# Where the searches for the 256 keys stand in a two-layer attention trunk

## The chip, the core and the metric

The kernel runs on one core of one Trainium2 chip. The metric is device time in microseconds (us). Before the change three runs took 4272.74, 4274.78 and 4277.41 us; their median is 4274.78 us. TensorE is called PE here, VectorE DVE, ScalarE ACT, GpSimd POOL, and SP issues all DMAs.

## What is computed

The reference is two layers of one mixer over 2048 tokens of width 1024. Each layer normalises its rows, projects them, feeds four head groups of width 256 and maps their gated results back:

```python
h = rms_norm(x, ln_g)
proj = jnp.einsum('bsd,dn->bsn', h, w_in)
y_a = stick_breaking(a_q, a_k, a_v)                    # group A
y_b = softmax_attention(q_b, k_b, v_b, MLA_QK ** -0.5) # group B, latent attention
y_c = dsa_attention(qc, kc, c_v, iq, ik, iw, topk)     # group C, 256 chosen keys
y_d = rms_norm(diff_attention(...), diff_subln_g) * (1.0 - lam_init)  # group D
x = x + einsum(concat(silu(gate) * y), w_out)
```

In group C the keys of a query are chosen by an index score, and only the 256 best take part:

```python
score = jnp.einsum('bqh,bqhs->bqs', iwb, jax.nn.relu(logits))
score = jnp.where(adm[None], score, -jnp.inf)
top_val, top_idx = lax.top_k(score, kn)                # kn = min(256, keys)
```

## The kernel before

Tokens are cut into 16 tiles of 128. A layer is seven sweeps over these tiles, in the order `a h d0 d1 b c o`: stick-breaking with the index scores (a), the latents and two gates of group B (h), differential attention in two halves (d0, d1), latent attention (b), attention over the chosen keys (c), and the output projection (o). Within a sweep, tile t is attended while tile t+2 is prepared (transposes of its q and k) and tile t+3 is projected; the weights of the next sweep are asked for four and five tiles ahead. A scheduler then puts every engine's instructions in a fixed order, which the engine follows: an instruction that waits holds all that stand behind it on the same engine.

An attention sweep takes a tile in units (one head or a pair of heads). A unit's scores come from PE into PSUM; DVE masks and scales them into a row buffer and takes the minimum (`att_row`, L841 and L843), ACT takes the exponentials (L847); PE transposes the rows, DVE or ACT copy them out of PSUM, and PE multiplies with v (`att_pv`, L283 and L866). In d0 and d1 the differences of two rows are formed in between (L1066 to L1074).

The choice of the 256 keys (`ci_search`, from L516) works on a group of tiles at once. For each tile, ACT counts the scores above a threshold with one activation over the whole row (L538); then a chain of 21 small DVE instructions on columns of all tiles of the group sets the next thresholds (L601 to L622). There are two counts before the loop and eight rounds in it. At the end each tile takes four long DVE instructions over its row (L630, L632, L633, L640). Where the table `SEARCH` names two groups at one place, their rounds are interleaved. The table's key says at which sweep and tile the searches are started:

```python
SEARCH = {("a", 4): ((2, 3),), ("a", 7): ((4, 5),), ("a", 10): ((6, 7),),
          ("a", 15): ((8, 9), (10, 11)), ("h", 3): ((12, 13), (14, 15))}
```

A search may not be late: the mask of tile i is read in sweep c. Its score rows (`sg`, 4 bytes for each key, so 5632 bytes in each partition for tile 10 and 8192 for tile 15) lie in one of two rings of memory. A ring hands out its space in the order of the program and waits until whatever lay there has been read for the last time:

- `rows` (30,720 bytes) holds the scores of sweep a, the `sg` rows of tiles 2 to 13, and the row buffers `rw` of all attention sweeps.
- `ring` (88,832 bytes) holds weights, keys and values, and the `sg` rows of tiles 14 and 15 (`INBIG`).

Weights arrive in slices of 128 rows (k = 0 to 7) through two buffers (`w_raw`, L216); ACT and DVE, or POOL, split each slice into a high part `w_hi` and a low part `w_lo` in `ring`. `proj` (L256, L257, L260) multiplies with them, three passes over eight slices.

Of the kernel before, what the change touches and what calls it, by code (L numbers as in the profile page):

```python
# [18 lines left out]
PSUM = bass.MemoryType.PSUM  # L19
# [18 lines left out]
SEARCH = {("a", 4): ((2, 3),), ("a", 7): ((4, 5),), ("a", 10): ((6, 7),), ("a", 15): ((8, 9), (10, 11)), ("h", 3): ((12, 13), (14, 15))}  # L38
# [22 lines left out]
def merge(*gens):  # L61
    """Interleaves generators, whose first item is their whole cost and whose others are costs of steps."""
# [27 lines left out]
class Share:  # L90
    """A generator taken in shares of its cost."""
# [16 lines left out]
class Trunk:  # L108
# [53 lines left out]
    def g2(self, shape, dtype=F32):  # L162
        """scratch of the projections, up to 2 KB"""
        return self.wk.tile(shape, dtype, name="g2", bufs=4)

    def pt(self, shape, dtype=F32):
        """scratch of the attention's inner loops, up to 2 KB"""
        return self.wk.tile(shape, dtype, name="pt", bufs=3)

    def o2(self, shape, dtype=F32):  # L170
        """scratch of the attention's results, up to 2 KB"""
        return self.wk.tile(shape, dtype, name="o2", bufs=2)
# [22 lines left out]
    def split(self, hi, lo, raw, eng="pp"):  # L195
        """hi: raw rounded, lo: what that leaves"""
# [9 lines left out]
    def weights(self, W, key, src, pieces, n, kt=KT, first=False):  # L206
        """src [kt*128, cols] in DRAM; pieces (column, count) side by side make n columns."""
# [3 lines left out]
        for k in range(kt):  # L211
            # the very first ones come all at once, through the memory of the rows
# [15 lines left out]
    def early(self, i, n):  # L228
        """who splits: ScalarE and VectorE while the attention of tile i leaves them time, else GpSimd"""
# [33 lines left out]
    def rstd(self, who, ss, n, width):  # L263
        """(ss / width + eps) ** -0.5 of [128, n]"""
# [10 lines left out]
    def transposes(self, dst, srcs, eng="act", tag="pj"):  # L275
        """srcs: up to four [128, m] fp32 views; dst [m, len, 128] view."""
# [3 lines left out]
        # sources of rounded results are rounded themselves  # L280
# [8 lines left out]
    def piece(self, st, key, i, shape, dtype=F32):  # L289
        """the tile of key that holds token tile i, of four each; last but one dim of shape is 4 tiles long"""  # L290
# [5 lines left out]
    def at(self, offset, g):  # L296
        """generator g, its instructions scheduled as if they came offset instructions later"""
# [17 lines left out]
    def a_load(self, l, i, st):  # L315
        """x tile -> normalised, transposed, split"""
# [41 lines left out]
    def functions_a(self):  # L358
        """has ScalarE take the set of functions with both exponential and logarithm"""
        self.nc.scalar.preload_act_table_set("natural_log_exp_and_others")  # L360

    def a_first(self, l, i, st):
# [33 lines left out]
        for r in range(2):  # L396
# [6 lines left out]
            if zr is not None:  # L403
                # what is left of the stick after these blocks is at most exp(X0 - z0)
# [63 lines left out]
    def hilo64(self, u):  # L468
        """u [128, 5, 64]: [hi lo] of the first four, [hi hi] and [lo lo] of the last"""
# [9 lines left out]
    def ci_score(self, l, i, st, tied=True):  # L479
        """scores of tile i into a row buffer"""  # L480
# [3 lines left out]
        # the general search takes two more rows  # L484
# [3 lines left out]
        for c0 in range(0, n, 512):  # L488
            w = min(512, n - c0)
            # equal scores of zero rank by their index  # L490
# [25 lines left out]
    def ci_search(self, l, b):  # L516
        """per row of the tiles of b a threshold with 249..256 scores at or above it, then the 256th itself"""
# [17 lines left out]
        def count(dst, th):  # L535
            """number of scores at or above th"""
# [24 lines left out]
        # threshold among the zeros: bracket (-(n + 0.5) TINY, Z) .. (0.5 TINY, P0)  # L561
# [13 lines left out]
        # above zero  # L575
# [9 lines left out]
        # below zero  # L585
# [12 lines left out]
        for it in range(NITER):  # L598
# [16 lines left out]
            # outside the bracket: its middle  # L615
# [8 lines left out]
        # the 256th of each row: 256 - count below the threshold found  # L624
# [64 lines left out]
    def ga_att(self, l, i, st):  # L689
        """stick-breaking of query tile i over every key block"""  # L690
# [54 lines left out]
    def gc_search(self, l, i, st):  # L745
        """the 256 greatest scores of each row, equal ones by lowest index: bit by bit"""
# [712 lines left out]
```

## Time and profile before

| | |
|---|---|
| median of three runs | 4274.78 us |
| the profiled execution, span | 4276.6 us |
| PE busy | 3937.6 us (92%) |
| DVE busy | 2906.3 us (68%) |
| ACT busy | 2371.9 us (55%) |
| POOL busy | 1650.7 us (39%) |
| mean granted clock of PE | 0.957 |

The page cuts the span into 40 slices and shows for each the busy share of an engine in tenths. PE stands at 8 or 9 in most slices; the ones with 7, at a granted clock of 7 to 9 tenths, are few and lie at the same places in both layers. Around these places the windows below are cut. Busy time is the union of an engine's instructions. A granted clock between 0.5 and 1 in a window is a mean over stretches at PE's two levels, 1.2 and 2.4 GHz. The profiled execution is one run; its span is 1.8 us above the median of the timed ones.

Landmarks of layer 0, in us from the start of the span: sweep a to about 473, h from 435 to 647, d0 from 662 to 1000, d1 to 1263, b to 1636, c to 1960, o to 2139. Layer 1 repeats this about 2125 us later.

### The profile page before, as it was taken

The numbers are of one execution on the slowest core, as the hardware profiler recorded it, in microseconds if no ns is written. First come the engines' busy times: TensorE is split into PE (matmuls) and PEld (weight loads), VectorE is DVE, ScalarE is ACT, GpSimd is POOL, SyncE is SP. The second block draws the span as 40 slices with busy tenths as digits, with TensorE's granted clock in tenths as the row PEclk, the third lists the DMA queues.
The fourth block names the chain that finished last, engine by engine and source line by source line (L and its number), as shares of the span: only waits on it lengthen the run. The fifth ranks groups of instructions, "written<-read, shape, count | busy, mean of one in ns | idle before, by whom it ended". The sixth has DMA issues, their size and how long they took to land.

```text
span 4276.6 us, 75274 instructions
## 1 busy us (share of the span) xinstructions
PE 3937.6 (92%) x25833; PEld 3249.9 (76%) x25833; DVE 2906.3 (68%) x10326; ACT 2371.9 (55%) x4846; POOL 1650.7 (39%) x2350
## 2 busy tenths in 40 slices
PE   6999996899988999999989999979999889999999
PEld 6877786777866777777878787867788667777777
DVE  3798788787875655663337988887968766555622
ACT  3656677465665545454126667765666655554621
POOL 2333423665664433420033343337747544344100
PEclk9999997899988999999999999979999899999999
DMA  3222531121110002114522225311211100021144
GB/s 104 80 77 84 175 112 58 50 59 52 50 35 26 19 23 68 50 44 139 167 88 81 81 91 172 114 54 48 61 53 49 36 22 18 26 74 46 59 138 139
DMA packets 204842, 312.60 MB, mean 73 GB/s; under 512 B 63777, under 2 KB 147873, under 8 KB 203937
## 3 DMA queue, kind: packets, MB, share of 16 engines
q1 hardware_dynamic: 204448, 307.69, 22.7%
q8 instruction: 206, 3.38, 0.3%
q14 instruction: 188, 1.53, 0.1%
HBM read 211.89 MB, written 95.72 MB: 72 GB/s over the span
## 4 chain that ended last, share of the span: by engine, by line
PE 57%; DVE 20%; ACT 6%; POOL 6%; DMA 5%; issue 5%; SPq 0%; DVEq 0%; ACTq 0%; POOLq 0%
PE y L866 9%; PE s L837 8%; PE tp L283 7%; PE pj L256 7%; PE pj L257 6%; PE pj L260 6%; PE s L256 3%; PE s L257 3%; PE s L260 3%; ACT junk L538 2%; DVE sc L506 2%; DVE rw L843 2%; PE pj L283 2%; DMA w_raw<-w_in 2%; DVE rw L841 2%
## 5 line engine op out<-in xcount | busy, mean ns | idle before, releaser
L256 PE MATMUL pj<-w_hi,h_hi 128*128 128x384 f32 (+4 forms) x2560 | 880.2, 352 | 51.5 <-POOL w_hi L193 22.9
L257 PE MATMUL pj<-w_lo,h_hi 128*128 128x384 f32 (+4 forms) x2560 | 863.9, 345 | 8.0 <-DVE w_lo L204 4.0
L847 ACT ACTIVATE rw<-rw,at_mn 128x896 f32<-128x896 f32 (+15 forms) x512 | 615.7, 1204 | 173.1 <-DVE at_mn L846 148.2
L285 ACT COPY pt<-tp 128x512 f32<-128x512 f32 (+3 forms) x689 | 358.1, 529 | 467.8 <-PE tp L283 390.3
L256 PEld LDWEIGHTS pj<-w_hi,h_hi 128*128 128x128 f32 x2560 | 505.7, 198 | 88.9 <-POOL w_hi L193 26.0
L283 PE MATMUL tp<-ident,rw 128*128 128x128 f32 x3264 | 540.4, 287 | 34.4 <-DVE rw L1074 20.3
L257 PEld LDWEIGHTS pj<-w_lo,h_hi 128*128 128x128 f32 x2560 | 505.3, 197 | 32.4 <-DVE w_lo L204 6.6
L260 PE MATMUL pj<-w_hi,h_lo 128*128 128x384 f32 (+4 forms) x2560 | 523.4, 338 | 0.0
L283 PEld LDWEIGHTS tp<-ident,rw 128*128 128x128 f32 x3264 | 365.4, 143 | 172.2 <-issue 117.5
L843 DVE TENSOR_SCALAR_CACHE_REDUCE rw<-s 128x512 f32<-128x512 f32 x576 | 383.0, 684 | 108.2 <-PE s L837 73.7
L260 PEld LDWEIGHTS pj<-w_hi,h_lo 128*128 128x128 f32 x2560 | 434.1, 190 | 25.7 <-issue 10.8
L271 POOL TENSOR_SCALAR rs<-ss 128x2 f32<-128x2 f32 (+4 forms) x224 | 61.7, 276 | 802.8 <-DVE ss L987 202.7
L538 ACT ACTIVATE junk<-sg,st_T 128x1152 int8<-128x1152 f32 (+4 forms) x224 | 293.9, 1312 | 83.9 <-DVE st_T L622 56.9
L272 POOL TENSOR_TENSOR rs<-rs,mhalf 128x8 f32<-128x8 f32 (+5 forms) x256 | 317.0, 1239 | 16.9
L287 DVE COPY pt<-tp 128x512 f32<-128x512 f32 (+3 forms) x247 | 152.9, 619 | 197.6 <-PE tp L283 163.5
L837 PE MATMUL s<-dk,qa 96*128 96x512 f32 (+3 forms) x640 | 233.5, 424 | 43.9 <-DVE rw L843 22.3
L187 POOL TENSOR_TENSOR h_lo<-x4a,h_hi 128x1024 fp32r<-128x1024 f32 x103 | 255.5, 2480 | 39.4 <-PE pj L260 22.8
L193 POOL TENSOR_SCALAR hl<-g 128x256 fp32r<-128x256 f32 (+1 forms) x384 | 151.2, 408 | 286.9 <-DVE g L452 61.3
L837 PE MATMUL s<-bk,qa 128*128 128x512 f32 (+6 forms) x960 | 257.8, 394 | 1.2 <-DVE at_mn L841 0.7
L283 PE MATMUL pj<-identr,hl 128*128 128x128 f32 (+1 forms) x1280 | 174.6, 258 | 74.1 <-POOL hl L187 47.9
L193 POOL TENSOR_SCALAR h_hi<-x4a 128x1024 fp32r<-128x1024 f32 x103 | 115.2, 1119 | 319.8 <-PE pj L257 156.1
L841 DVE CUSTOM_DVE_ANT_0 rw<-s,maskR 128x128 f32<-128x128 f32 (+3 forms) x400 | 187.7, 478 | 56.7 <-PE s L837 55.5
(267 smaller groups left out, 8731.5 us busy)
## 6 DMA issues: line engine op xcount, KB each, us to landing
x4a<-hT SPq DMA_DIRECT2D x128, 512.0 KB, 3.5
x4a<-x SPq DMA_DIRECT2D x32, 512.0 KB, 3.5
hT<-x4a SPq DMA_DIRECT2D x32, 512.0 KB, 2.6
x4a<-y SPq DMA_DIRECT2D x32, 512.0 KB, 3.5
x4b<-gate SPq DMA_DIRECT2D x32, 512.0 KB, 3.6
x4c<-x SPq DMA_DIRECT2D x32, 512.0 KB, 4.1
y<-o SPq DMA_DIRECT2D x96, 128.0 KB, 2.1
w_raw<-w_in SPq DMA_DIRECT2D x48, 192.0 KB, 2.6
```

The source lines that it names most:

```text
L256: nc.tensor.matmul(p[:, :n], hi[:, k, :], whi[k], start=(k == 0), stop=False)
L257: nc.tensor.matmul(p[:, :n], hi[:, k, :], wlo[k], start=False, stop=False)
L260: nc.tensor.matmul(p[:, :n], lo[:, k, :], whi[k], start=False, stop=(k == kt - 1))
L272: nc.gpsimd.tensor_tensor(r, r, self.mhalf[:, :n], op=OP.pow)
L283: nc.tensor.transpose(p[:m, j, :].bitcast(dst.dtype), s.bitcast(dst.dtype), ident)
L285: nc.scalar.copy(dst, p[:m, :len(srcs), :])
L538: nc.scalar.activation(self.junk[:, :ns[g]], Sg[g], AF.Sign, bias=th[:, g:g + 1], scale=-1.0, accum_out=dst[:, g:g + 1])
L837: nc.tensor.matmul(p[:, :w], x, y, start=(k == 0), stop=(k == len(ops) - 1))
L841: nc.vector.tensor_tensor_reduce(o, p[:, :w], b, -scale, 3.0e38, OP.add, OP.min, m)
L843: nc.vector.tensor_scalar(o, p[:, :w], -scale, None, op0=OP.mult, op1=OP.min, accum_out=m)
L847: nc.scalar.activation(rw, rw, AF.Exp, bias=mn, scale=-1.0, accum_out=ls)
L866: nc.tensor.matmul(y[o:o + 64, :], v(j), pt[:, c * m:(c + 1) * m, :].rearrange("p a b -> p (a b)"), start=(j < 2), stop=(j >= nb - 2), ski ...
```

## The change

Three things are edited. The first two are the table and a call in the projection of sweep b, which lets the table name places there:

```diff
-SEARCH = {("a", 4): ((2, 3),), ("a", 7): ((4, 5),), ("a", 10): ((6, 7),), ("a", 15): ((8, 9), (10, 11)), ("h", 3): ((12, 13), (14, 15))}
+SEARCH = {("a", 4): ((2, 3),), ("a", 7): ((4, 5),), ("a", 10): ((6, 7),), ("a", 15): ((8, 9),), ("h", 3): ((10, 11, 12, 13),), ("b", 4): ((14, 15),)}
...
     def proj_b(self, l, i, st):
         nc, wk = self.nc, self.wk
         yield 1600.0
+        self.search_at(l, "b", i)
         raw = self.g2([128, 3, 128])
```

The third takes out comments and docstrings, which leaves no trace in the program. Tiles 8 and 9 are now searched alone at the end of sweep a; tiles 10 to 13 are one group in sweep h; tiles 14 and 15 are a group that is named when tile 4 of sweep b is projected. Seven groups a layer become six. The `sg` rows of 14 and 15 still lie in `ring`, but they are asked for in sweep b, between the keys and values (`bk`, `bv`) of tiles 0 to 3 and those of tiles 4 to 7. The sizes are as before, so whatever is asked for later finds other neighbours under it.

How the fixed orders move is shown at three places. In each, `junk` is the discarded output of a count, `st_` are the small columns of a search, `rw` a row buffer, `pj`, `tp`, `s` and `y` are PSUM tiles.

ACT at the start of d0 in layer 0, before. The width tells the tile: 128x256 are the rows of tile 1 of d0, and 128x1664 to 128x2048 are counts of tiles 12 to 15.

```order
L847 ACTIVATE rw,d_l_8376<-rw,at_mn 128x256
L847 ACTIVATE rw,d_l_8377<-rw,at_mn 128x256
L200 CAST h_hi<-x4a 128x1024
L538 ACTIVATE junk,st_T<-sg,st_T 128x2048
L1167 COPY g_8284<-pj 128x256
L847 ACTIVATE rw,d_l_8376<-rw,at_mn 128x256
L847 ACTIVATE rw,d_l_8481<-rw,at_mn 128x256
L285 CAST qa<-pj 96x512
L285 COPY pt<-tp 128x256
L285 CAST dk<-pj 96x4x128
L538 ACTIVATE junk,st_T<-sg,st_T 128x1664
L538 ACTIVATE junk,st_T<-sg,st_T 128x1792
```

The same place after the change, from the last count of the search of tiles 10 to 13 (128x1792 is tile 13) to the second unit of tile 1.

```order
L538 ACTIVATE junk,st_T<-sg,st_T 128x1792
L981 COPY dv<-pj 128x128
L985 ACTIVATE x4b<-pj 128x256
L1093 ACTIVATE o_7922,ss<-y,at_rl 128x64 x2
L200 CAST h_hi<-x4a 128x1024
L1167 COPY g_7948<-pj 128x256
L285 CAST qa<-pj 96x512
L285 CAST dk<-pj 96x4x128
L981 COPY dv<-pj 128x128
L985 ACTIVATE x4b<-pj 128x256
L200 CAST h_hi<-x4a 128x1024
L1167 COPY g_8121<-pj 128x256
```

Before, tile 1's four rows stood close together and the search ran on behind them, to tile 3. Now the search ends between tile 1's two units, and the projections of two later tiles stand ahead of the second unit.

PE at the end of sweep b in layer 0, before. `pj<-w_hi,h_hi 128x384` is the projection of a tile of sweep c, `bk` and `bv` are keys and values of sweep b. These are the last rows of c's first projection and what follows it.

```order
L257 MATMUL pj<-w_lo,h_hi 128x384
L260 MATMUL pj<-w_hi,h_lo 128x384 x4
L283 MATMUL tp<-ident,rw 128x128
L260 MATMUL pj<-w_hi,h_lo 128x384
L866 MATMUL y<-pt,bv 64x128 x4
L283 MATMUL tp<-ident,rw 128x128
L260 MATMUL pj<-w_hi,h_lo 128x384 x3
L283 MATMUL tp<-ident,rw 128x128 x4
L837 MATMUL s<-bk,qa 128x512 x3
L866 MATMUL y<-pt,bv 64x128 x2
```

After the change: the same projection, which has got as far as its fifth slice much earlier, goes on here, behind the very last values of sweep b (L878 closes tile 15).

```order
L283 MATMUL tp<-ident,rw 128x128 x4
L257 MATMUL pj<-w_lo,h_hi 128x384
L256 MATMUL pj<-w_hi,h_hi 128x384
L866 MATMUL y<-pt,bv 64x128 x4
L257 MATMUL pj<-w_lo,h_hi 128x384
L866 MATMUL y<-pt,bv 64x128 x4
L256 MATMUL pj<-w_hi,h_hi 128x384
L878 MATMUL y<-both,o_20111 128x64 x4
L257 MATMUL pj<-w_lo,h_hi 128x384
L256 MATMUL pj<-w_hi,h_hi 128x384
L257 MATMUL pj<-w_lo,h_hi 128x384
L260 MATMUL pj<-w_hi,h_lo 128x384 x8
```

Before, c's first three projections stood between b's last tiles. Now the first of them breaks off at slice 4 and ends behind b's last tile, and the next two stand behind it.

DVE in sweep b in layer 0, before, around the copies of tile 2's results (L888) and the projection of a later tile (L1207 to L1217).

```order
L1207 TENSOR_REDUCE ss<-g_16007 128x4
L841 ISA rw,at_mn<-s,maskR 128x384
L841 ISA at_mn 128x1
L888 TENSOR_TENSOR o_16241<-y,at_rl 128x256
L287 COPY pt<-tp 128x384
L886 RECIPROCAL at_rl<-at_l 128x4
L1213 SCALAR_TENSOR_TENSOR g_16017<-pj,rs,gain_r 128x32 x4
```

About the same place after the change.

```order
L622 COPY_PREDICATED st_T<-st_nd,st_sp 128x2
L630 TENSOR_SCALAR ge,st_T<-sg,st_T 128x1920
L632 SCALAR_TENSOR_TENSOR sg<-ge,sg 128x1920
L634 TENSOR_SCALAR st_rc<-st_T 128x1
L888 TENSOR_TENSOR o_16192<-y,at_rl 128x256
L633 MAX st_ex<-sg 128x8
L636 TENSOR_SCALAR st_oh<-iota_221,st_rc 128x9
L1206 TENSOR_REDUCE ss<-g_15947 128x4
L1207 TENSOR_REDUCE ss<-g_15947 128x4
```

The search of tiles 14 and 15 is now strung between the instructions of b's first five tiles and, before those, of d1's last three.

## Rows read from the trace of the kernel before

**Rows 1.** The page: the span and its instructions, busy time of each engine.

```profile
span 4276.6 us, 75274 instructions
PE 3937.6 (92%) x25833; PEld 3249.9 (76%) x25833; DVE 2906.3 (68%) x10326; ACT 2371.9 (55%) x4846; POOL 1650.7 (39%) x2350
```

**Rows 2.** Windows: start:end, length, engines' busy us, PE's clock, DMA share, GB/s.

```profile
663.80:825.30 161.50, 126.40 (x768) 112.55 (x766) 134.03 (x560) 96.56 (x211) 79.02 (x110) 0.81 0.17 51
1006.10:1105.30 99.20, 95.62 (x714) 85.65 (x713) 74.34 (x283) 63.99 (x172) 58.11 (x96) 1.00 0.20 59
2788.80:2951.00 162.20, 123.93 (x768) 109.93 (x766) 132.58 (x553) 98.28 (x211) 80.34 (x110) 0.82 0.17 51
3124.70:3227.10 102.40, 98.82 (x715) 88.84 (x713) 74.38 (x283) 64.04 (x172) 58.11 (x96) 0.97 0.20 58
1202.80:1263.60 60.80, 50.60 (x328) 36.58 (x326) 54.21 (x185) 42.46 (x79) 32.49 (x48) 0.83 0.09 24
1263.60:1337.40 73.80, 58.25 (x383) 46.65 (x380) 34.34 (x120) 35.24 (x99) 33.69 (x59) 0.79 0.12 34
1569.00:1627.00 58.00, 58.00 (x449) 47.62 (x448) 29.94 (x91) 26.71 (x43) 17.30 (x22) 1.00 0.11 35
```

**Rows 3.** Timeline of ACT: first exponential of tiles 0 and 8, d0 and d1.

```profile
663.85 0.39 ACT L847 ACTIVATE rw<-rw,at_mn 128x128 f32<-128x128 f32 x1
...
825.26 1.26 ACT L847 ACTIVATE rw<-rw,at_mn 128x1152 f32<-128x1152 f32 x1 [1.58 <-DVE at_mn L846]
...
1006.08 0.40 ACT L847 ACTIVATE rw<-rw,at_mn 128x128 f32<-128x128 f32 x1 [2.41 <-DVE at_mn L841]
...
1105.35 1.26 ACT L847 ACTIVATE rw<-rw,at_mn 128x1152 f32<-128x1152 f32 x1
```

**Rows 4.** Groups of DVE's search instructions within 663.8 to 825.3 us.

```profile
L640 DVE SCALAR_TENSOR_TENSOR ge<-sg,st_sp,ge 128x1664 int8<-128x1664 f32 (+3 forms) x4 | 8.6, 2143 | 0.0
...
L606 DVE COPY_PREDICATED st_L<-st_up,st_T 128x4 f32<-128x4 int32 x10 | 1.8, 179 | 0.0
...
L618 DVE TENSOR_TENSOR st_up<-st_sp,st_L 128x2 f32<-128x2 f32 x10 | 1.7, 169 | 0.2
```

**Rows 5.** Groups of PE within 635 to 663 us, where d0 starts.

```profile
L256 PE MATMUL pj<-w_hi,h_hi 128*128 128x384 f32 (+1 forms) x17 | 7.1, 435 | 9.9 <-POOL w_hi L193 7.1 <-ACT w_hi L200 2.8
L257 PE MATMUL pj<-w_lo,h_hi 128*128 128x384 f32 (+1 forms) x15 | 6.4, 441 | 3.4 <-DVE w_lo L204 2.3 <-POOL w_lo L187 1.1
```

**Rows 6.** Groups by form over the span: counts, a round's accumulators, long instructions.

```profile
L538 ACT ACTIVATION_READ_ACCUMULATOR junk<-sg,st_T 128x1 f32 x224 | 43.4, 194 | 0.0
L538 ACT ACTIVATE junk<-sg,st_T 128x2048 int8<-128x2048 f32 x16 | 32.1, 2008 | 0.1
L538 ACT ACTIVATE junk<-sg,st_T 128x1920 int8<-128x1920 f32 x16 | 30.4, 1899 | 2.6 <-DVE st_md L616 1.8 <-DVE st_T L622 0.6
...
L640 DVE SCALAR_TENSOR_TENSOR ge<-sg,st_sp,ge 128x2048 int8<-128x2048 f32 x2 | 4.7, 2334 | 0.0
...
L630 DVE TENSOR_SCALAR_CACHE_REDUCE ge<-sg,st_T 128x1408 int8<-128x1408 f32 x2 | 3.4, 1680 | 0.1
```

**Rows 7.** Timeline of DVE and ACT in d0: tile 4 and tile 13's last instructions.

```profile
746.26 0.83 ACT L847 ACTIVATE rw<-rw,at_mn 128x640 f32<-128x640 f32 x1 [3.73 <-DVE at_mn L846]
...
753.38 2.08 DVE L640 SCALAR_TENSOR_TENSOR ge<-sg,st_sp,ge 128x1792 int8<-128x1792 f32 x1
...
759.56 0.84 ACT L847 ACTIVATE rw<-rw,at_mn 128x640 f32<-128x640 f32 x1
```

**Rows 8.** Timeline around 2891 us: POOL and DVE.

```profile
2890.91 2.36 POOL L187 TENSOR_TENSOR h_lo<-x4a,h_hi 128x1024 fp32r<-128x1024 f32 x1
...
2891.39 4.03 DVE L632 SCALAR_TENSOR_TENSOR sg<-ge,sg 128x2048 f32<-128x2048 int8 x1
```

**Rows 9.** Timeline, 1574 to 1590 us: projection of c's tile 0 and its transposes.

```profile
1574.43 0.41 PE L256 MATMUL pj<-w_hi,h_hi 128*128 128x384 f32 x1
...
1579.03 0.77 PE L260 MATMUL pj<-w_hi,h_lo 128*128 128x384 f32 x3
...
1590.08 0.55 PE L283 MATMUL pj<-identr,hl 128*128 128x128 f32 x5
```

## The prediction

> **What bounds the kernel now.** I read the page first: PE is busy for 92% of the span [rows 1], so in most of the program another engine's work is free as long as it keeps pace. What can move the time are the places where PE is not fed. I then cut windows around the dips of the clock. The clearest pair is d0 against d1, the same work twice: from the first exponential of tile 0 to that of tile 8, d0 takes 161.5 us and d1 99.2; in layer 1 it is 162.2 and 102.4 [rows 2, 3]. PE does about as many matmuls in both, yet in d0 its clock is granted at 0.81 and it idles for 35 us. The only extra work in d0's stretch is the search of tiles 12 to 15: DVE is busy 134.0 - 74.3 = 59.7 us longer, ACT 96.6 - 64.0 = 32.6. So there the search is not hidden at all: 62 us a layer for 60 us of DVE work. Ten rounds of small instructions and the long ones of four tiles are in it [rows 4].
>
> Three boundaries matter, in order of time: h to d0, d1 to b, b to c. All terms are for one layer until the sum.
>
> **h to d0, a gain.** Two things change.
>
> (1) The search. The long instructions of tiles 12 to 15 are about 4 x 8.5 = 34 us of the 59.7 [rows 4], so ten rounds are 25.7, 2.6 us each. That a small instruction on four columns takes as long as one on two (179 and 169 ns) [rows 4] makes a group of four as cheap a round as a group of two. In ACT's new order the last count stands between tile 1's two units: about 2.5 rounds remain behind d0's first exponential instead of ten, 6.5 us. The long ones of tiles 10 to 13 go over 50 blocks of keys instead of 58: 29.5 us. That leaves 36 us of DVE work in the stretch. In proportion to the price above, 62.3 x 36 / 59.7 = 37.6, which saves 25. If DVE's share is what holds, (74.3 + 36) us at the 83% it reached (134.0 of 161.5) is 133 us, which saves 29. A third reading goes by the ring `rows`: the second row of tile 4 in d0 lies on tile 13's scores. Before, that search instruction was issued at 753.4 us and took 2.1, and the row's exponential came at 759.6, 13 us behind the row ahead of it [rows 7]. A search that ends a round or two past tile 0 would free it about 40 us earlier. But the same ring now makes tile 1's third row wait for tile 10, which was long free before, and tiles 2 and 3 for 11 and 12. I take 30.
>
> (2) Weights. From h's gain to the end of d0's first weights 1664 + 26,624 + 32,768 + 15,872 + 512 + 24,576 = 102,016 bytes were asked for, 13 KB more than `ring` has; so d0's slices from the low part of the fourth on waited until h's tile 15 was done, and PE idled 9.9 + 3.4 = 13.3 us for their splits [rows 5]. Without the 15,872 bytes of scores all of the first weights fit, and seven of the narrow gate slices stay late. I take 8 of the 13.
>
> Sum: -38. Ends: -9, if the longer group ends no sooner against d0, and -71, if d0 falls to d1's pace and the weights are free.
>
> **d1 to b, a loss.** Tiles 14 and 15 bring 20 counts of 1.90 and 2.01 us with 0.19 for each accumulator, 43 us of ACT [rows 6]. On DVE there are eight rounds of 2.6, a set-up worth two, and eight long instructions of about 2.3 [rows 6]: 21 + 5 + 18 = 44 us. By the order, 11 counts and four rounds with the set-up stand ahead of b's first exponential. There, over d1's last three tiles, DVE is busy 54.2 of 60.8 us and ACT 42.5 [rows 2]. With 23 us more ACT needs 66, with some 15 more DVE 69; at the 90% that DVE reaches there that is 77, so up to 16 us, and I take 13. The rest, 29 us of DVE, falls into b's first 73.8 us, where only 34.3 are taken [rows 2]; it fits, but in DVE's order long instructions stand ahead of a projection's reductions (the third place of the order), behind which POOL's splits and PE's transposes wait. I take 9. Sum +22. Ends: +5, which is ACT's overload alone, and +44, d0's price of one for one. Below nothing is excluded, since here work is only added.
>
> Where POOL and DVE meet I weigh one rule. The same long instruction on 2048 columns, reading two operands, took 4.03 us while a POOL subtraction of 2.36 us was running, where its like takes 2.3 [rows 6, 8]. The Trainium skill, page "SBUF — State Buffer", section "Who interferes with whom", says that a DVE instruction with two SBUF operands and a GpSimd one that reads SBUF shut each other out for a whole instruction. The trace agrees in this one place, with 1.7 us. It speaks against the change, since b's transposes wait for POOL's splits.
>
> **b to c, a loss.** This is where the scores of 14 and 15 now lie. From b's first values to the end of c's weights, `ring` is asked for 4 x 14,336 (`bk` and `bv`) + 15,872 + 1024 + 24,576 = 98,816 bytes, 10 KB too many; without the scores it was 82,944 and fitted. So c's slices from about the fifth on (with what is lost at the ring's end, from the fourth in layer 1) lie on `bv` and `bk` of tiles 0 to 3, and these are read until tile 15's last head. That is what PE's order shows: c's first projection breaks off and ends behind b's last tile. Before, PE was busy for all of the 58 us from 1569 to 1627, and c's projections filled it [rows 2]. Their matmuls are moved, 24 for each tile, and cost nothing by that: b ends earlier by as much. What is new is that nothing else lies beside c's first chains. From the end of the first projection (1579.8) to its transposes (1590.1) 10.3 us passed, hidden under b [rows 9]; part was POOL's other work, so I count 8. By the new order the transposes stand directly behind the projection, ahead of the next one. Then come tile 0's minima and exponentials (3), and the same for tile 1 and 2 with a projection between (2 + 3 + 2), and the last slices, which are two loads behind (2 in layer 0, 5 in layer 1): 20 and 23 us. Starved like this at b's start PE was granted 0.79 [rows 2]; on some 25 us of work that is 5 more. Sum: +25 and +28. Ends: +5, if the order's slack takes the chains, and +47, which is what PE lost over d1's end and b's start by idling and clock, 60.8 - 0.83 x 50.6 and 73.8 - 0.79 x 58.3 [rows 2].
>
> **The sum.** 2 x (-38 + 22) + 25 + 28 = +21 us on the profiled 4276.6. That run stood 1.8 above the median, so 4296. In the rest of sweep h I count nothing: PE is the engine there, and the one group fewer takes work off DVE that it hid.
>
> **Rivals.**
>
> *d0 falls to d1's pace (faster).* Its delay before is a chain through the ring `rows`, not a sum of work: once tile 13's scores are free in time nothing holds d0. For it: the 13 us between tile 4's rows. Against it: the long instructions stay in DVE's way, and tile 1 has a new wait. Price -70 for -38: 2 x (-70 + 22) + 53 = -43, 4232. It decides once that stretch of d0, with the weights, is 48 us shorter than before.
>
> *The gap before c is filled.* Its stalls cost 5, for instance since b's tail waits less with the projections gone: 2 x (-38 + 22 + 5) = -22, 4253. For it: 449 matmuls in 58 us left no room. Against: PE's order.
>
> *The search is only spread out.* The lone group of four waits for its counts where two groups filled each other's gaps; it ends no sooner, and d0 keeps all but 15 us of its delay, while b pays one for one: 2 x (-15 + 44) + 53 = +111, 4386. The change would then not take the search out of d0 at all. For it: the new wait of tile 1. Against: half the rounds in d0.
>
> *POOL shut out.* Four long two-operand instructions, 1.7 us each, in b's path: +7 a layer, 4310.
>
> **Numbers.** A measurement of this kernel tells 0.2%, 9 us, from no change. Chances: my forecast 0.40 (its own range 4275 to 4320), d0 at d1's pace 0.20, gap filled 0.14, only spread out 0.15, POOL 0.11. Of the forecast I give 0.09 to no change and 0.31 to slower; of the first two rivals, which end on the other side, 0.31 to faster and 0.03 to no change; the last two are slower. That is slower 0.57, same 0.12, faster 0.31. The range goes from 4230, near the first rival, to 4358, short of the third.
>
> **What would show it.** Right: d0's stretch of tiles 0 to 7 near 130 us; the gap between tile 1's units in d0 ended by a search instruction on tile 10; PE without idle for weights between h and d0's first transposes; d1's last three tiles and b's first four together some 20 us longer; in the last tile of b no projection, and behind it c's first tiles with PE idle for POOL's splits and a clock below 1. Wrong: d0's stretch at 105 us or still at 150; c's first three tiles fed without such idling; b's start unchanged.

## The result: 3% slower

The changed kernel took 4410.09 us (median of 4 runs, 4403.93 to 4414.08), the one before 4275.40 beside it. The ratio is 1.0308, with a 95% interval of 1.0293 to 1.0322. The forecast was 4296 us, with a range up to 4358. The direction was right; the loss is 135 us instead of 21.

The page of the kernel after, first two rows, beside [rows 1]:

```profile
span 4409.5 us, 74789 instructions
PE 4006.5 (91%) x25833; PEld 3289.2 (75%) x25833; DVE 2884.4 (65%) x9902; ACT 2372.2 (54%) x4846; POOL 1651.0 (37%) x2350
```

PE does the same 25,833 matmuls and is busy 69 us longer; the span is 133 us longer. About half of the loss is PE's idling (64 us more), the other half that the same matmuls kept it busy longer, at a mean granted clock of 0.941 where it was 0.957. To find the places, I read ACT's first exponential of each tile off the timelines (as in [rows 3]) and cut both executions at the same tiles. Times in us, layer 0 and layer 1:

| stretch | before | after | difference | forecast |
|---|---|---|---|---|
| up to d1's tile 0 (layer 1: from c's end) | 1006.1 / 1171.8 | 996.0 / 1166.5 | -10.1 / -5.3 | -38 / -38 |
| d1, tile 0 to 12 | 166.9 / 170.0 | 167.0 / 175.1 | +0.1 / +5.1 | 0 |
| d1's tile 12 to b's tile 4 | 164.5 / 164.1 | 195.5 / 185.3 | +31.0 / +21.2 | +22 / +22 |
| b, tile 4 to 8 | 73.3 / 73.7 | 73.4 / 72.0 | +0.1 / -1.7 | 0 |
| b's tile 8 to c's tile 4 | 274.9 / 272.8 | 318.6 / 316.3 | +43.6 / +43.4 | +25 / +28 |
| c's tile 4 to its end | 267.2 / 264.4 | 266.0 / 270.4 | -1.2 / +6.0 | 0 |

Windows of the kernel after; the columns are those of [rows 2]. In order: d0's tiles 0 to 7, d1's last three tiles, b's first four, b's end, the gap before c's first exponential, c's first four tiles.

```profile
659.60:810.50 150.90, 116.90 (x730) 103.08 (x728) 112.48 (x397) 77.15 (x189) 80.34 (x108) 0.84 0.15 47
1194.90:1266.80 71.90, 55.64 (x317) 38.50 (x317) 60.80 (x265) 59.30 (x96) 28.16 (x39) 0.79 0.05 13
1266.80:1358.50 91.70, 68.13 (x389) 53.14 (x390) 70.67 (x274) 50.98 (x117) 34.32 (x63) 0.71 0.09 27
1580.00:1639.30 59.30, 58.84 (x487) 44.49 (x486) 31.17 (x89) 29.63 (x44) 1.51 (x5) 1.00 0.03 9
1639.30:1676.80 37.50, 23.47 (x176) 18.75 (x175) 12.70 (x26) 9.84 (x22) 15.79 (x18) 0.82 0.29 94
1676.80:1750.40 73.60, 58.69 (x272) 44.65 (x272) 29.23 (x100) 25.80 (x66) 26.39 (x43) 0.77 0.17 51
```

The first row: DVE is busy 112.5 us in d0's stretch, 38 more than in d1's of before [rows 2]. That is the 36 us of search that the forecast left there, yet the stretch fell only from 161.5 to 150.9. The fourth and fifth rows: POOL works 1.5 us in b's last 59 us, and PE is idle for 14 of the 37.5 us behind them.

The timeline of that place, one row for each step (start, length, engine, line, operation, count; in brackets the idle time before and what ended it):

```profile
1580.01 0.82 SPq L216 DMA_DIRECT2D w_raw<-w_in  x1
...
1637.25 2.00 ACT L847 ACTIVATE rw<-rw,at_mn 128x2048 f32<-128x2048 f32 x1 [0.97 <-DVE at_mn L846]
...
1648.20 0.88 SPq L216 DMA_DIRECT2D w_raw<-w_in  x2
...
1650.77 0.51 POOL L193 TENSOR_SCALAR w_hi<-w_raw 128x384 fp32r<-128x384 f32 x1 [69.27 <-DMA w_raw<-w_in]
...
1664.73 0.62 POOL L193 TENSOR_SCALAR w_hi<-w_raw 128x512 fp32r<-128x512 f32 x1 [1.91 <-DMA w_raw<-w_out]
1665.32 0.67 POOL L193 TENSOR_SCALAR hl<-g 128x256 fp32r<-128x256 f32 x2
1665.95 1.26 POOL L187 TENSOR_TENSOR w_lo<-w_raw,w_hi 128x512 fp32r<-128x512 f32 x1
1667.17 1.65 POOL L187 TENSOR_TENSOR hl<-g,hl 128x256 fp32r<-128x256 f32 x2
1667.95 1.29 PE L283 MATMUL pj<-identr,hl 128*128 128x128 f32 x6 [12.27 <-POOL hl L187]
...
1676.77 0.40 ACT L847 ACTIVATE rw<-rw,at_mn 128x128 f32<-128x128 f32 x1 [0.52 <-DVE at_mn L841]
```

From 1580 to 1648 no weight is loaded. POOL stands 69 us in front of one slice, and all that stands behind it in POOL's order stands too. When b's last head has read the first values, a late slice of c, slices of o's weights (128x512), the split of a further h and then those of c's first queries and keys (`hl`) go through POOL one after the other, and PE idles 12.3 us for `hl`.

The search in sweep h, on DVE: the end of each round, and the last long instruction on tile 13.

```profile
600.61 0.15 DVE L622 COPY_PREDICATED st_T<-st_nd,st_sp 128x4 f32<-128x4 int32 x1
613.65 0.17 DVE L622 COPY_PREDICATED st_T<-st_nd,st_sp 128x4 f32<-128x4 int32 x1
...
654.37 0.17 DVE L622 COPY_PREDICATED st_T<-st_nd,st_sp 128x4 f32<-128x4 int32 x1
669.08 0.17 DVE L622 COPY_PREDICATED st_T<-st_nd,st_sp 128x4 f32<-128x4 int32 x1
684.22 0.17 DVE L622 COPY_PREDICATED st_T<-st_nd,st_sp 128x4 f32<-128x4 int32 x1
698.34 0.15 DVE L622 COPY_PREDICATED st_T<-st_nd,st_sp 128x4 f32<-128x4 int32 x1
...
752.47 2.07 DVE L640 SCALAR_TENSOR_TENSOR ge<-sg,st_sp,ge 128x1792 int8<-128x1792 f32 x1
```

A round of the lone group takes 13 to 15 us, since chain and counts wait for each other, and the search of tile 13 ends at 754.5 us: before it was 755.5 [rows 7]. Before, tile 15 was still to come; its last long instruction, from the timeline of DVE before:

```profile
775.82 2.33 DVE L640 SCALAR_TENSOR_TENSOR ge<-sg,st_sp,ge 128x2048 int8<-128x2048 f32 x1
```

So the search as a whole now ends 24 us sooner, that of tile 13 does not.

### The profile page after: what moved, and what is told of

Same layout as the page of the kernel before. It is cut to its first block, busy times and chain, and to the rows that moved or that the text cites. A ratio compares the mean times of both kernels' runs of the same rounds, so it can differ in the third digit from the quotient of the medians.

```text
span 4409.5 us, 74789 instructions
## 1 busy us (share of the span) xinstructions
PE 4006.5 (91%) x25833; PEld 3289.2 (75%) x25833; DVE 2884.4 (65%) x9902; ACT 2372.2 (54%) x4846; POOL 1651.0 (37%) x2350
## 5 line engine op out<-in xcount | busy, mean ns | idle before, releaser
L283 PE MATMUL tp<-ident,rw 128*128 128x128 f32 x3264 | 557.5, 293 | 66.7 <-DVE rw L1074 25.7
L260 PEld LDWEIGHTS pj<-w_hi,h_lo 128*128 128x128 f32 x2560 | 435.3, 191 | 25.5 <-issue 10.6
L538 ACT ACTIVATE junk<-sg,st_T 128x1408 int8<-128x1408 f32 (+5 forms) x224 | 293.4, 1310 | 118.1 <-DVE st_T L622 101.8
L283 PE MATMUL pj<-identr,hl 128*128 128x128 f32 (+1 forms) x1280 | 177.7, 263 | 72.3 <-POOL hl L187 45.7
```

The costliest lines, as they stand in the source:

```text
L260: nc.tensor.matmul(p[:, :n], lo[:, k, :], whi[k], start=False, stop=(k == kt - 1))
L283: nc.tensor.transpose(p[:m, j, :].bitcast(dst.dtype), s.bitcast(dst.dtype), ident)
L538: nc.scalar.activation(self.junk[:, :ns[g]], Sg[g], AF.Sign, bias=th[:, g:g + 1], scale=-1.0, accum_out=dst[:, g:g + 1])
```

## The experiments

All are timed beside the kernel before on the same chip; the table gives stretches of the profiled executions, layer 0 / layer 1. "Rows" are the score rows `sg`. A stretch is read from one execution; that of "held back" is the slowest of its ten, 9 us above their median. The diffs are cut to the lines that matter and shortened; they are against the kernel after, those of "held and early", "held, four" and "d0 clear" against "held back".

| run | us | d0, tiles 0 to 7 | d1's 12 to b's 4 | b's 8 to c's 4 |
|---|---|---|---|---|
| before | 4275 | 161 / 162 | 165 / 164 | 275 / 273 |
| after | 4410 | 151 / 145 | 196 / 185 | 319 / 316 |
| ring only | 4364 | 160 / 171 | 166 / 154 | 314 / 317 |
| rows first | 4340 | 148 / 144 | 189 / 196 | 276 / 287 |
| two pairs | 4403 | 142 / 146 | 192 / 195 | 317 / 317 |
| only 14, 15 | 4390 | 142 / 151 | 195 / 186 | 314 / 315 |
| held back | 4268 | 144 / 142 | 161 / 161 | 279 / 295 |
| held and early | 4297 | 149 / 154 | 165 / 160 | 277 / 297 |
| held, four | 4296 | 148 / 146 | 161 / 160 | 279 / 302 |
| d0 clear | 4419 | 133 / 137 | 166 / 163 | 278 / 295 |
| b and c | 4284 | 133 / 130 | 156 / 164 | 271 / 277 |
| no margin | 4322 | 132 / 131 | 160 / 161 | 289 / 294 |
| swap | 4267 | 146 / 146 | 155 / 162 | 279 / 276 |

**Ring only.** The space without the search.

```diff
-SEARCH = {... ("a", 15): ((8, 9),), ("h", 3): ((10, 11, 12, 13),), ("b", 4): ((14, 15),)}
+SEARCH = {... ("a", 15): ((8, 9), (10, 11)), ("h", 3): ((12, 13), (14, 15))}
...
-        self.search_at(l, "b", i)
+        if i == 4: # two rows in self.ring, filled by DMA, nc.vector.max over [:, ::32]
```

> The searches stand as in the kernel before, all of them; only the space is taken: at tile 4 of sweep b two rows of 7168 and 8192 bytes are asked for in ring, filled from DRAM and read once by a small DVE instruction (128 of its columns). Theory R (memory): the space alone, lying between b's keys and values, pushes c's weights from the fifth slice on (fourth in layer 1) onto bv and bk of tiles 0 to 3, and that is the whole stall between b and c. Then about 44 us a layer are lost, as after against before: c's first exponential 37 to 41 us behind b's last instead of 0.5, and 4275 + 88 = 4363 us, 4345 to 4375. Theory W (work): the stall comes from the search work in b, which makes the projections of c late. Then the time stays within 10 us of 4275.

4364.20 us, ratio 1.0214 (1.0197 to 1.0231): theory R. That the sum fits to a microsecond is luck in part: between b's tile 8 and c's tile 4 39 and 44 us are lost, and shifts of up to 16 us elsewhere cancel. (The first row has 7680 bytes, as in the prediction's 15,872; the 7168 of the expectation is a slip.) The window of the gap, and the timeline around it:

```profile
1614.40:1653.10 38.70, 24.04 (x177) 19.41 (x176) 15.38 (x39) 10.45 (x23) 18.12 (x21) 0.82 0.29 97
```

```profile
1612.35 2.00 ACT L847 ACTIVATE rw<-rw,at_mn 128x2048 f32<-128x2048 f32 x1 [0.70 <-DVE at_mn L846]
...
1625.88 0.51 POOL L193 TENSOR_SCALAR w_hi<-w_raw 128x384 fp32r<-128x384 f32 x1 [69.21 <-DMA w_raw<-w_in]
...
1642.22 1.00 PE L283 MATMUL pj<-identr,hl 128*128 128x128 f32 x6 [11.76 <-POOL hl L187]
...
1653.09 0.40 ACT L847 ACTIVATE rw<-rw,at_mn 128x128 f32<-128x128 f32 x1
```

The same stall with the same waits (69.2 and 11.8 us), and no search near it. Two thirds of the loss are where two rows lie.

**Rows first.** The converse: after's searches, but the space is asked for ahead of b's first values, and the search takes those rows.

```diff
+        if i == 0: self.early_sg = [self.ring.tile([128, 128 * (j + 1)], F32, name="sg") for j in INBIG]
         self.search_at(l, "b", i)
```

> As after, with the same searches at the same places, but the space of the score rows of tiles 14 and 15 is asked for at tile 0 of sweep b, ahead of b's first keys and values. Nothing of c's weights then lies on what b still reads. Theory R: c's first exponential is again within 2 us of b's last, and of after's 4410 some 88 us go: 4322, 4310 to 4340. What is left over before, about 45 us, is then the price of the search work at d1's end and b's start (29 us a layer) less the 8 that d0 gave. Theory W: no more than 10 us go, 4400 to 4410.

4339.99 us (ratio 1.0147, 1.0123 to 1.0170): 70 us go, not 88. Layer 0 is as expected (c's first exponential 0.5 us behind b's last); in layer 1 14.5 us stay between them. There 4736 bytes are lost at the ring's end, and c's first keys (`ck`) come to lie on b's first values. From b's first values to c's first keys 88,064 bytes are asked for, 768 fewer than the ring has. The last three runs take this up.

**Two pairs.** Is it the lone group's slowness that holds d0?

```diff
-("h", 3): ((10, 11, 12, 13),)
+("h", 3): ((10, 11), (12, 13))
```

> As after, but tiles 10 to 13 are two groups of two, (10, 11) and (12, 13), started at the same place and interleaved. Same counts, same long instructions, twice as many small DVE instructions. Theory L (latency): a group alone waits for its four counts and then for its own chain of small instructions, 13 to 15 us a round, and d0's rows wait in memory for the search to end on tiles 10 to 13; two groups fill each other's gaps. Then the search ends some 30 us sooner (last long instruction on tile 13 near 725 instead of 754), d0's stretch of tiles 0 to 7 is near 125 us instead of 151, and the time is 4410 - 50 = 4360, 4340 to 4385. Theory D (DVE's share): what holds d0 is the amount of DVE work beside it; then the doubled small instructions make it the same or worse, 4405 to 4425.

4403.08 us. The search ends 32 us sooner, as theory L has it; its last instruction on tile 13 (the timeline of DVE):

```profile
720.78 2.07 DVE L640 SCALAR_TENSOR_TENSOR ge<-sg,st_sp,ge 128x1792 int8<-128x1792 f32 x1
```

But d0's stretch falls by 8.5 us in layer 0 and not at all in layer 1. So the end of the search is worth little in d0: the stretch was to be near 125 us and the time 4360. The time is 2 us under theory D's range, but the stretch got shorter, which D does not have; neither theory holds as it stands.

**Only 14 and 15.** The last part of the change alone.

```diff
-("a", 15): ((8, 9),), ("h", 3): ((10, 11, 12, 13),), ("b", 4): ((14, 15),)
+("a", 15): ((8, 9), (10, 11)), ("h", 3): ((12, 13),), ("b", 4): ((14, 15),)
```

> The last part of the change alone: tiles 8 to 11 are searched as before at the end of sweep a, in two groups; tiles 12 and 13 alone in sweep h, and tiles 14 and 15 at tile 4 of sweep b. Theories R and L: b and c lose what they lose in after, 29 + 44 us a layer; in d0 one group of two with rounds of 8 to 9 us ends near 715 instead of 755, so d0 gives back 30 to 40 us a layer. 4275 + 146 - 70 = 4351, 4335 to 4375. If d0's delay is DVE's amount of work, d0 has 15 us of search left and falls to d1's pace, 50 us a layer: 4320. If neither (d0's delay is not the search's at all), 4410 or more.

4389.82 us (ratio 1.0271, 1.0254 to 1.0288). The losses in b and c are after's; d0 gives 19 and 12 us, not 30 to 40. So even with one group of two left, which ends 64.6 us behind d0's first exponential, where before's search ended 115 behind it, d0's stretch stays above 140. The time lies between the prices of the expectation (4351, 4320, 4410 or more).

**Held back.** Rows first, and the search kept from starting: each row gets one column of tile 7's values of sweep b copied into it before its load.

```diff
+        if ("b", i) in SEARCH:
+            for r in self.early_sg:
+                nc.vector.tensor_copy(r[:, 0:1], st["bv"][i // 4][:, i % 4, 0:1])
+            self.search_at(l, "b", i)     # ("b", 7): ((14, 15),), searches of 8 to 13 as in the run above
```

> Tiles 8 to 11 at the end of sweep a in two groups, tiles 12 and 13 in sweep h (all as in the run with 14 and 15 alone), the space of 14 and 15 asked for ahead of b's first keys, and their search held back until tile 7 of sweep b is projected, by a copy of one column of that tile's values into each row before it is filled. There, in b's tiles 5 to 9, PE is busy for nearly all of the time and DVE for about two thirds in before. Theory P (place): a search costs nothing where PE is the engine and DVE has room; then b's start is as before (d1's tile 12 to b's tile 4 within 5 us of 164), b's tiles 4 to 15 within 10 us of 295, and the time is 4275 - 2 x 26 = 4223, 4210 to 4245. Rival A (amount): 44 us of DVE and 43 of ACT cost what they cost in after, 29 us a layer, wherever they stand: 4281 or more.

4267.92 us, ratio 0.9982 (0.9972 to 0.9991): not 4223, since d0 gave less than 26 a layer and in layer 1 the 14.5 us before c stayed and d1 is 7 us longer than before; nor is it rival A's 4281 or more. The gain of 8 us is within the 9 that the prediction takes for no change. Theory P holds for the search itself nearly, at 7 us a layer instead of nothing. The window of b's tiles 4 to 7 in both layers, where the search begins (in layer 0 8 of its 47 us on DVE lie here, the rest in b's later tiles):

```profile
1315.60:1393.50 77.90, 70.58 (x549) 55.22 (x547) 55.38 (x244) 57.58 (x115) 30.86 (x58) 1.00 0.14 45
3428.70:3504.10 75.40, 68.67 (x543) 54.40 (x541) 53.51 (x235) 55.25 (x112) 30.95 (x58) 1.00 0.14 47
```

and the same tiles before:

```profile
1337.40:1410.80 73.40, 67.78 (x536) 53.76 (x535) 47.97 (x177) 43.69 (x99) 30.84 (x58) 1.00 0.08 20
```

With the clock at 1.00 throughout, the stretch is 4.5 and 1.7 us longer (in layer 1 it was 73.7); d1's end and b's start, which lost 31 and 21, are back at 161. The same work that cost 31 and 21 us at b's start costs 7 a layer in its middle (from tile 4's first to tile 15's last exponential: 295.4 us before, 302.4 here; in layer 1 292.5 and 299.5).

**Held and early.**

```diff
-("h", 3): ((12, 13),)
+("h", 1): ((12, 13),)
```

> As the run before it, and the search of tiles 12 and 13 starts at tile 1 of sweep h, so that it ends before d0's first exponential: no search instruction is left in d0. Theory S (search): the 62 us by which d0's first eight tiles exceed d1's are the search; then d0's stretch falls to 99 to 112 us, and the time is 30 to 40 us a layer below the run before: about 4155. Theory F (filling): d0 follows a sweep without attention, so its first tiles wait for the chain projection, POOL, transposes, with nothing beside it; then the stretch stays at 130 to 142 us whatever the search does, and the time is within 20 us of the run before.

4296.92 us, and a miss of mine: named earlier, tiles 12 and 13 only pushed 10 and 11 back; tile 11's last long instruction came at 736.7 us, and DVE was busy with the search in d0 more than in the run before. It tells nothing on the question of d0 without a search.

**Held, four.** After's groups without the rest of its losses.

```diff
-("a", 15): ((8, 9), (10, 11)), ("h", 3): ((12, 13),)
+("a", 15): ((8, 9),), ("h", 3): ((10, 11, 12, 13),)
```

> The groups of after, (8, 9) alone and 10 to 13 as four, with 14 and 15 as in the two runs before: space first, search held back to tile 7 of sweep b. It shows the price of the group of four by itself. Theory L (latency): its eight rounds of 13 to 15 us end with tile 13 near 754 and hold d0's rows in memory, so d0 is as in after, 8 us a layer better than before, and the time is 15 to 20 us a layer above the run with 12 and 13 alone: 4260, 4245 to 4275. Theory D (DVE's amount decides in d0): the same amount is left in d0 to within 8 us, and the two runs agree within 15 us.

4295.86 us, 28 above the held-back run: the group of four with a lone (8, 9) costs 14 us a layer against the pairs. In the profiled executions 4 of it are in d0's stretch in each layer; the rest is spread over other sweeps and not explained (in layer 0 d0 even begins 7 us sooner). Theory L's 15 to 20 us a layer nearly came, but not in d0, where it had them; theory D's agreement within 15 us did not.

**d0 clear.** No search in d0's first eight tiles at all.

```diff
-("h", 3): ((12, 13),)
+("d0", 11): ((12, 13),)      # and self.search_at(l, f"d{st['half']}", i) in proj_d
```

> As the held-back run, with tiles 8 to 11 again searched at the end of sweep a, but tiles 12 and 13 are named at tile 11 of sweep d0, so that their search starts when d0 is at tile 8: none of it can lie in d0's first eight tiles (the run meant for this had left 51 to 57 us of search there). Theory S: the 62 us by which d0's stretch exceeds d1's are the search. Then the stretch falls from 144 to 99 to 112 us. Theory F (filling): about half of the 62 us are the price of a sweep that starts with nothing beside its first chains of projection, POOL and transposes. From the stretches seen so far (161 us with 76 us of summed DVE search time in it, 142 with 34) a straight line gives 127 at none; 120 to 135. The time: the search now lies in d0's tiles 8 to 11, where DVE has less room than in b; a loss of 5 to 15 us a layer there against a gain of 10 to 25: 4250, 4230 to 4275; by theory S 4200 to 4230.

Windows of d0's tiles 0 to 7 in both layers, and of the rest of d0 in layer 0:

```profile
656.50:789.20 132.70, 116.00 (x740) 101.33 (x738) 77.15 (x285) 62.65 (x170) 72.34 (x109) 0.90 0.16 49
2836.00:2972.90 136.90, 119.81 (x739) 105.14 (x737) 77.43 (x285) 62.78 (x170) 72.23 (x109) 0.86 0.15 47
789.20:1049.40 260.20, 185.59 (x1226) 148.84 (x1227) 194.01 (x686) 144.84 (x254) 112.94 (x144) 0.82 0.15 45
```

DVE is busy 77 us, as in d1 (74) [rows 2], and the stretch is 133 and 137 us, not 99: theory S falls. The size is theory F's (layer 1 is 2 us outside its range); that the filling is the reason, this run does not show. PE idles 17 us in layer 0 and runs at a clock of 0.90 with no search beside it. The time was forecast badly (4419 instead of 4250): the rows of 12 and 13 fill 13.8 KB of `rows` while d0's own buffers are long, and tiles 8 to 15 took 260 us for 181. The waits of that stretch (engine, line, what was waited for, us in total, times, longest) name it: PE stands before scores that DVE has not yet been able to write to a row buffer.

```profile
PE s L840 <- DVE rw L846: 34.7, 15, 18.7
```

**b and c, no margin.** Tiles 12 and 13 in b, 14 and 15 in c; with and without a margin at the ring's end.

```diff
+("b", 7): ((12, 13),), ("c", 5): ((14, 15),)        # held back in b and c as above
+ ... self.ring.tile([128, 128 * (j + 1) + p], ...)  # p = 512 or 928 columns at j = 12; 0 in the second run
```

> Tiles 8 to 11 searched as before at the end of sweep a. Tiles 12 and 13 lie in ring ahead of b's first keys and are held back to tile 7 of sweep b; tiles 14 and 15 are asked for in ring at tile 5 of sweep c and held back to that tile's values. No search is left in h, d0 or d1. The first row of 12 and 13 is made wider (2048 bytes in layer 0, 3712 in layer 1, never used), so that c's first keys end just below b's first values. Theories R (memory), P (place) and F (filling) together: d0 as in the run with d0 clear, 20 us (layer 0) and 14 us (layer 1) better than the held-back run; b's and c's start as in before in both layers, also in layer 1, where 14.5 us between b and c had been left (c's first keys lay on bv of tile 0); c's tiles 4 to 15 at most 5 us a layer longer. 4268 - 34 - 15 + 5 = 4224, 4205 to 4250. If a search costs its amount wherever it stands, c loses 25 us a layer: 4265 or more.

> As the run before it without the wider row: c's first keys (tiles 0 to 3) then lie on bv of b's tiles 0 to 3 in both layers, by 1920 bytes in layer 0 and 2944 in layer 1. Theory R: these 2 to 3 KB alone keep c's first keys waiting for b's last values, 10 to 18 us a layer between b's last and c's first exponential, and the time is 20 to 35 us above the padded run. Rival: so small an overlap, of keys and not of weights, is hidden by c's own filling; the two runs agree within 8 us.

4284.00 and 4321.58 us. The two differ by 37.6 us, by 2 to 3 KB of overlap; theory R again, now with keys in place of weights. Both have 129.5 to 133 us in d0's stretch. What failed was mainly c, where the search was to be nearly free. Window of c's tiles 4 to 14 in layer 0 with it, and before:

```profile
1669.50:1926.10 256.60, 243.62 (x1660) 177.38 (x1658) 191.34 (x713) 164.16 (x262) 83.14 (x110) 0.99 0.16 55
```

```profile
1685.70:1928.20 242.50, 236.34 (x1643) 174.90 (x1643) 146.99 (x471) 127.25 (x223) 81.77 (x108) 0.99 0.16 50
```

DVE takes 44 us more, and the stretch is 14 us longer, though DVE had 95 us free in it; in layer 1 it is 20 us longer (258.8 for 238.7). Besides, d0's second half in layer 0 took 196 us, where it was 177 in held back; why, stays open.

**Swap.** 14 and 15 back in h as before, 12 and 13 in b, with a margin in layer 1 only.

```diff
+("a", 15): ((8, 9), (10, 11)), ("h", 3): ((14, 15),), ("b", 7): ((12, 13),)
```

> Tiles 8 to 11 at the end of sweep a and tiles 14 and 15 at tile 3 of sweep h, both as in before; only tiles 12 and 13 leave d0: their rows lie in ring ahead of b's first keys (in layer 1 the first one 2944 bytes wider, never used, so that c's first keys end below b's first values), and their search is held back to tile 7 of sweep b. Theory P with R: d0 has one group of two, whose rows lie in ring and not in the way of d0's row buffers, and loses 15 to 20 us a layer against before as in the held-back run or more; b's and c's starts are as in before in both layers; b's tiles 4 to 15 at most 8 us a layer longer. 4275 - 2 x 18 + 2 x 5 = 4249, 4230 to 4262. If the search in b costs what it gives back in d0: 4268 to 4280.

4266.71 us, ratio 0.9985 (0.9976 to 0.9994), the best with the held-back run. It is short of the 4249 that was expected, and 0.15% better than before, which the prediction would call no change. The layer-1 stall is gone (0.2 us), d0 gives 15 and 16 us, b and c take some of it.

## Why the prediction was wrong

**h to d0: -38 forecast, -10 and -5 measured.** The step that failed is the first one, "so there the search is not hidden at all: 62 us a layer for 60 us of DVE work". (The stretch at 150 us, a sign of being wrong, came in layer 0.) Two numbers that agree were read as cause and effect. Without any search d0's stretch is 130 to 137 us in six measurements (two layers of three kernels), so 25 to 33 of the 62 us hang on the search; the rest, some 30 us, is d0's own, and PE's clock there is 0.86 to 0.93.

The sentence before it, "the only extra work in d0's stretch is the search", was wrong by its own rows: POOL was busy 79.0 us there and 58.1 in d1 [rows 2], and without a search it is still busy 72.3. In d0's stretch POOL splits the h of five tiles, in d1's of one, where ACT and DVE split the others. From the groups of POOL in d0 clear and in d1 of before (count, busy us, mean ns, idle time before), and PE's waits in the same two stretches:

```profile
L187 POOL TENSOR_TENSOR h_lo<-x4a,h_hi 128x1024 fp32r<-128x1024 f32 x5 | 12.0, 2401 | 0.1
L187 POOL TENSOR_TENSOR h_lo<-x4a,h_hi 128x1024 fp32r<-128x1024 f32 x1 | 2.4, 2400 | 0.7 <-PE pj L260 0.7
```

```profile
PE pj L283 <- POOL hl L187: 10.2, 8, 2.6
PE pj L283 <- POOL hl L187: 2.8, 6, 0.9
```

Of the 17 us that PE idles in d0 clear, 10.2 are for POOL's `hl`. The filling of the first tiles cannot be all of it: in that run, layer 0, tiles 0 to 3 take 62 us for d1's 45, and tiles 4 to 7 70 for 55. Which of the two, POOL's splits or the start behind a sweep without attention, starves PE no run tells apart; this stays open.

The amounts were right (36 us of DVE work left, 38 found); the price of one for one was not: 22 us less work gave 10.6 us in layer 0, 24 gave 17 in layer 1. Even without a search no kernel came near d1's pace, so the rival "d0 at d1's pace" fell.

The weights' term came true as a wait but not as time. PE's waits for the splits, 13.3 us before [rows 5], are 4.5 in the last 28.6 us ahead of d0's first exponential in layer 0 of after (its groups of PE; 1.1 of the first row is a wait for `g`):

```profile
L256 PE MATMUL pj<-w_hi,h_hi 128*128 128x384 f32 (+2 forms) x32 | 11.8, 379 | 4.5 <-ACT w_hi L200 3.4 <-ACT g L1167 1.1
L257 PE MATMUL pj<-w_lo,h_hi 128*128 128x384 f32 (+2 forms) x32 | 11.7, 375 | 1.1 <-POOL w_lo L187 0.8 <-DVE w_lo L204 0.3
```

Yet d0 began only 4.2 us sooner there, and 0.3 in two pairs and in only 14 and 15, where these waits shrink much the same (to 6.8 and 5.4). In layer 1 d0 began 11 us later behind c: sweep a ended 8 us later (by its last matmul for an index score) and sweep h took 3 us longer, stretches for which the forecast had put nothing; the cause is not known.

**The lone group of four.** "About 2.5 rounds remain" was read from the order and came true (the rounds that end at 669, 684 and 698), and still tile 13's search ended no sooner than before, where it was to free its row some 40 us earlier. The order says what stands behind what, not when. The new wait of tile 1 came as well: its second unit's exponentials start at 709.6 us, behind tile 10's last long instruction, which ends at 705.6, and from tile 1 to tile 2 it took 31 and 30 us, for 21 and 19 before. Both belong to the rival "only spread out", whose 4386 was the nearest price, in part by luck: it has 44 us a layer at b's start, where 31 and 21 were measured, and 53 in both layers together before c, where 87 were. And the pairs, which end 32 us sooner, show that this end is worth 8.5 us in d0 at most; that rival is right in the fact and wrong in what it decides.

**d1 to b: +22 forecast, +31 and +21 measured.** Right in place and nearly in size, though of the 13 and 9 us that were forecast for d1's last three tiles and b's first four, 11 and 18 came in layer 0 and 7 and 11 in layer 1. That it is the place and not the amount, the held-back run shows. "POOL shut out" cost little, because the two seldom met: of the eight long two-operand instructions in after's sweep b two had a POOL instruction beside them, and none got longer. Once POOL did instead. The kernel after, timelines of DVE and POOL: the same two splits, first beside a long instruction with one operand (L633), then, in layer 1, beside one with two (L632):

```profile
1350.89 2.29 DVE L633 MAX8 st_ex<-sg 128x8 f32<-128x2048 f32 x1
1351.07 0.61 POOL L193 TENSOR_SCALAR qb<-g 128x256 fp32r<-128x256 f32 x2 [4.51 <-DVE g L1043]
...
3530.72 2.28 DVE L632 SCALAR_TENSOR_TENSOR sg<-ge,sg 128x2048 f32<-128x2048 int8 x1
3530.88 2.89 POOL L193 TENSOR_SCALAR qb<-g 128x256 fp32r<-128x256 f32 x2 [1.97 <-DVE g L1043]
```

In [rows 8] POOL had started first, and DVE's instruction took 1.7 us longer than its like; here DVE had started first, and POOL's took 2.3 us longer. The rule cited from the Trainium skill, page "SBUF — State Buffer", section "Who interferes with whom", agrees with both places.

**b to c: +25 and +28 forecast, about +43.5 each measured.** The mechanism was right and is shown by ring only and rows first; the term was sized too small. That b ends earlier by the projections that are moved, came true: from its tile 8 to its last exponential 207.5 us for 222.0. I counted c's own first chains (20 and 23 us) and 5 for the clock. What I left out is what stands behind the waiting slice in POOL's order: 69 us without work there, then o's weights among c's first splits, so that the wait for `hl` is 12.3 us instead of 8, and c's tiles 0 to 3 take 73.6 us instead of 52.4 at a clock of 0.77.

Adding up: 28 and 33 us too much gain in d0, 19 and 16 too little loss before c, and 9 at b's start in layer 0 make some 104 of the 112 us by which the forecast was short; the rest is in d1 and c of layer 1 (+5 and +6).

## What to carry to other kernels

Moving work in a program that hands out memory in order moves the memory too: sum the bytes from the first buffer that is read late to the last one that must be early, loss at the ring's end included, before pricing the work; here 10 KB too many cost 39 to 44 us a layer and 2 to 3 KB cost 17. When a stretch is slow and extra work lies in it, look at every engine's row, not only at the one that is expected, and find the same stretch without the work before calling one the price of the other. Extra work on a side engine cost least here in the middle of sweep b, where PE was busy nearly all the time, and most where b starts; that such a middle is cheap is no rule, as sweep c shows. If its place is set by when its inputs are free, hold it back by an input.

## What was not expected

- Naming the search of 14 and 15 later, at b's tile 4, did not hold it back: it began in d1's last three tiles. Only a copy into its rows from a late tile did. That its place comes from when its memory is free fits this, but is not shown by itself.
- The same search (44 us of DVE and 43 of ACT by the prediction's count) cost 21 to 31 us at b's start, 7 from b's tile 4 on, and 14 and 20 in c's tiles 4 to 14, though before PE was busy for 98 and 97% and DVE for 64 and 61% in the two middles (layer 0). Why c is dearer than b stays open.
